# Down products of 16 of 22 hidden tiles as seven products of quadrants, in two passes behind the gates and ups

## The chip, the cores and the metric

The kernel runs on one core of a Trainium2 chip. The metric is device microseconds of one execution, median of three runs. Five engines work side by side, each in the order of its own queue: TensorE (PE, with PEld for its weight loads), VectorE (DVE), ScalarE (ACT), GpSimd (POOL) and SyncE (SP), which issues most DMAs.

## The reference

Two layers over 512 tokens of width 1024; this case is about the feed-forward that ends each.

```python
        h = h + rmsnorm(mixed @ w_out[layer], ln_mix_post[layer])
        f = rmsnorm(h, ln_ffn_pre[layer])
        f = (jax.nn.silu(f @ w_ffn_gate[layer]) * (f @ w_ffn_up[layer])) @ w_ffn_down[layer]
        h = h + rmsnorm(f, ln_ffn_post[layer])
```

D_FF is 2816: 22 hidden tiles of 128. All is float32.

## The kernel before

**Products.** A float32 operand is split into a high part, cast by ACT (L239), and the rest, subtracted by DVE (L240); one product is three matmuls, high by high, low by high, high by low (L182 to L184). A raw weight tile holds 512 KB, four of them are in flight (L134, L157); split weights have eight places.

**Feed-forward.** `boundary` normalizes and turns the rows of h and makes the first two hidden tiles; `combined` (L973) makes the seven sums and parts of the activations. The other 20 tiles come in pairs, in the groups (2,8), (8,14), (14,18), (18,22) of L1093. Gate and up of a pair are one `Seven` each: the two tiles by the two halves of the model and the two halves of the tokens are quadrants, of which seven products, instead of eight, give the result (Strassen-Winograd). A product is 4 k-tiles x 3 matmuls of 256 columns. Four sums of weights (L1022 to L1027) and three of results (L1060 to L1063) are on DVE, four copies out of PSUM on ACT. `gate_rows` (L1108) and `up_rows` (L1114) make silu(gate) x up and split it. After each of the first three groups come its down products (L1164 to L1174), plain: per half of the model and pair of tiles 2 x 4 token blocks x 3 matmuls of 512 columns, added into the eight tiles `ys` (L1174). The last group is done in `tail_of` (L810) token block by token block with the norm that follows.

**Order.** The program order of each engine is the order of its queue; `behind` puts an instruction after others without a wait of its own. SP issues the loads in program order, each when its raw tile is free. POOL has the reciprocal square roots (L253) and four DMAs between attention tiles (L382). PSUM has eight banks under the tags mm (3), lg (3) and tr (2).

Of the kernel before, what the change touches and what calls it, by code (L numbers as in the profile page):

```python
# [7 lines left out]
F32 = mybir.dt.float32  # L8
# [34 lines left out]
def hybrid(ctx: ExitStack, tc: tile.TileContext, i: dict, out: bass.AP):  # L43
# [7 lines left out]
    pp = ctx.enter_context(tc.tile_pool(name="psum", bufs=3, space=PSUM))  # L51

# [78 lines left out]

    def loaded(src):

        raw = wp.tile([P, 1024], F32, tag="raw", name=name("raw"), bufs=4)  # L134
        last_load[0] = nc.sync.dma_start(raw, src)
        return raw
# [182 lines left out]
    h = cp.tile([P, KT, T], F32, name="h")  # L319
# [490 lines left out]
    def tail_of(xs, load, ys, eps=None, last=False):  # L810
# [8 lines left out]
        def tail(tb, halfway=None, ahead=None):  # L819
# [10 lines left out]
            for n, (dh, m0, m1) in enumerate(at):  # L830
# [7 lines left out]
                V.tensor_add(y, o[:, cols], y)  # L838
# [158 lines left out]
    last_sum = [None, None]  # L997

    class Seven:
# [5 lines left out]
        def __init__(self, xs, src, tag, rows):  # L1005
            self.xs, self.rows = xs, rows
            w1, w2 = loaded(src(0)), loaded(src(1))
            self.a = [w[:, d : d + 512] for w in (w1, w2) for d in (0, 512)]
            self.x, self.p = ps(tag, s="x"), ps(tag, (P, 256), s="a")
            self.q = ps(tag, (P, 256), s="e")  # L1010
            self.s1, self.s2 = prob("s1"), prob("s2")

        def parts(self, src):
            pair = pair_of_parts()
            split(src, *pair)
            return pair

        def sums(self):

            a11, a12, a21, a22 = self.a  # L1020
            self.s3 = temp("s3")
            V.tensor_add(self.s3, a11, a21)  # L1022
            self.w1 = self.parts(a11)
            V.tensor_add(a21, a21, a22)
            self.w2 = self.parts(a12)
            V.tensor_add(a11, a21, a11)
            V.tensor_add(a12, a11, a12)  # L1027

        def product(self, o, w, n, more=False):
            for k, w in enumerate(cut(w, P)):  # L1030
                mm3(o, w, self.xs[n][k], k == 0 and not more, k == KT // 2 - 1, more)

        def run(self, what):

            a11, a12, a21, a22 = self.a
            left, right = (slice(*c) for c in HALVES)
            s1, s2 = self.s1, self.s2
            if what == 1:
                self.product(self.p, self.w1, 0)
                A.copy(s1[:, left], self.p)  # L1040
            elif what == 2:
                self.product(self.x[:, left], self.w2, 2)
            elif what == 3:
                self.product(self.x[:, right], self.parts(a12), 5)
            elif what == 4:
                self.product(self.q, self.parts(a22), 4, True)
            elif what == 5:
                self.product(self.p, self.parts(a21), 6, True)
                last_sum[0] = A.copy(s1[:, right], self.p)
            elif what == 6:  # L1050
                self.product(self.p, self.parts(a11), 3, True)
                A.copy(s2[:, left], self.p)
            else:
                self.product(self.q, self.parts(self.s3), 1)
                A.copy(s2[:, right], self.q)

        def end(self):
            left, right = (slice(*c) for c in HALVES)
            s1, s2 = self.s1, self.s2
            V.tensor_add(s2[:, left], self.q, s2[:, left])  # L1060
            V.tensor_add(s2[:, right], self.p, s2[:, right])
            self.rows(1, s2)
            last_sum[1] = V.tensor_add(s1, self.x, s1)  # L1063
            self.rows(0, s1)

    def sevens(pair, plain_first):

        if not plain_first:
            for make in pair:
                u = make()  # L1070
                u.sums()
                for n in (1, 7, 2, 6, 4, 3, 5):
                    u.run(n)
                u.end()
            return
        us = []
        for make in pair:
            us.append(make())
            us[-1].sums()
            for n in (1, 2, 3):  # L1080
                us[-1].run(n)
        for some in ((7, 6), (4, 5)):
            for u in us:
                for n in some:
                    u.run(n)
        for u in us:
            u.end()

    def feed_forward(layer, phase, xp, meanwhile=None):

        nnorm = PairNorm()
        rb = rbc
        groups = ((2, 8), (8, 14), (14, 18), (18, 22))  # L1093
# [11 lines left out]

        gates = [None, None]

        def gate_rows(row, g):  # L1108

            V.tensor_mul(g, g, rb)  # L1110
            A.activation(g, g, AF.Silu, scale=-1.0 if row else 1.0)
            gates[row] = g

        def up_rows(row, u, fs):  # L1114
            if row:
                V.scalar_tensor_tensor(out=u, in0=u, scalar=-1.0, in1=gates[1], op0=ALU.mult, op1=ALU.mult)
# [381 lines left out]
```

## Time and profile before

| what | us |
|---|---|
| three runs | 1113.7, 1114.55, 1115.03 |
| median | 1114.55 |
| span of the profiled execution | 1111.4 |
| PE busy | 1100.8 |
| DVE busy | 893.7 |
| ACT busy | 660.5 |

The profile is of another execution than the runs; its span goes from the first to the last instruction, so it is a few us shorter than a run's time. Each view's times are us from the start of that span. A row of a timeline gives start, duration, engine, line, operation, what it writes and reads, and the shape; a row of the windows the stretch, its length, busy time and count of PE, PEld, DVE, ACT and POOL, granted clock, DMA share and GB/s. The matmul rows overlap: each is longer than the step to the next start.

### The profile page before, as it was taken

The page shows a single profiled execution, that of the slowest core. Times are in us where ns is not written, and L with a number is a line of the kernel's source. Part 1 is how long each engine was busy: PE and PEld are TensorE (multiplying, and loading weights), DVE is VectorE, ACT ScalarE, POOL GpSimd, SP SyncE. Part 2 cuts the span into 40 slices and gives each one's busy share as a digit, 9 for nine tenths or more (in the row PEclk, how much of TensorE's full clock was granted, in tenths as well). Part 3 has the DMA queues.
Part 4 walks back from the last instruction along what each step waited for, and adds up shares of the span by engine and source line. Part 5 has one row for each costly group of instructions (what it writes and reads, how often), then busy time and mean ns, then how long its engine had stood idle before and what let it go on. Part 6 is the DMA issues. An engine that isn't in the chain of part 4 may idle for free.

```text
span 1111.4 us, 19500 instructions
## 1 busy us (share of the span) xinstructions
PE 1100.8 (99%) x7382; PEld 1000.1 (90%) x7382; DVE 893.7 (80%) x1735; ACT 660.5 (59%) x1397; POOL 25.3 (2%) x42
## 2 busy tenths in 40 slices
PE   9999999999999999999999999999999999999997
PEld 7998889998899898998988898889999899899996
DVE  8889658997697597896987898858997697687875
ACT  8776468664365264577665667668665265254553
POOL 0100000000000000001000000000000000000000
PEclk9999999999999999999999999999999999999999
DMA  7522322334133323343322654422224133333222
GB/s 267 162 76 77 98 74 76 115 109 141 57 112 97 117 92 114 97 148 117 104 88 62 173 132 116 131 76 74 79 90 154 62 114 96 101 109 114 77 76 76
DMA packets 64421, 118.12 MB, mean 106 GB/s; under 512 B 5260, under 2 KB 40088, under 8 KB 64328
## 3 DMA queue, kind: packets, MB, share of 16 engines
q1 hardware_dynamic: 63720, 116.18, 33.4%
q8 instruction: 58, 0.95, 0.4%
q0 software_dynamic: 192, 0.52, 0.2%
q14 instruction: 35, 0.29, 0.1%
q10 hardware_dynamic: 416, 0.18, 0.1%
HBM read 104.71 MB, written 2.10 MB: 96 GB/s over the span
## 4 chain that ended last, share of the span: by engine, by line
PE 94%; ACT 3%; DVE 1%; issue 1%; POOL 0%; DMA 0%; POOLq 0%; DVEq 0%; ACTq 0%
PE y L182 10%; PE y L183 10%; PE y L184 10%; PE a L182 5%; PE a L184 5%; PE a L183 5%; PE x L184 3%; PE e L182 3%; PE e L184 3%; PE e L183 3%; PE x L183 3%; PE x L182 3%; PE ps L184 3%; PE ps L183 3%; PE ps L182 3%; PE v L182 2%
## 5 line engine op out<-in xcount | busy, mean ns | idle before, releaser
L239 ACT CAST whi<-raw 128x512 fp32r<-128x512 f32 x460 | 273.1, 620 | 217.7 <-PE y L184 89.1
L240 DVE TENSOR_TENSOR wlo<-raw,whi 128x512 fp32r<-128x512 f32 x460 | 303.5, 684 | 69.5 <-ACT whi L239 67.8
L182 PE MATMUL y<-whi,fhi 128*128 128x512 f32 (+1 forms) x356 | 140.2, 394 | 0.4 <-DVE y L838 0.4
L184 PE MATMUL y<-whi,flo 128*128 128x512 f32 (+1 forms) x356 | 139.3, 391 | 0.0
L183 PE MATMUL y<-wlo,fhi 128*128 128x512 f32 (+1 forms) x356 | 139.2, 391 | 0.0
L184 PE MATMUL x<-xshi,wlo 128*128 128x256 f32 x320 | 89.9, 281 | 0.0
L182 PE MATMUL a<-xshi,whi 128*128 128x256 f32 x320 | 89.8, 281 | 0.0
L183 PE MATMUL x<-xslo,whi 128*128 128x256 f32 x320 | 89.7, 280 | 0.0
L182 PE MATMUL x<-xshi,whi 128*128 128x256 f32 x320 | 89.7, 280 | 0.0
L183 PE MATMUL a<-xslo,whi 128*128 128x256 f32 x320 | 89.7, 280 | 0.0
L184 PE MATMUL a<-xshi,wlo 128*128 128x256 f32 x320 | 89.6, 280 | 0.0
L184 PEld LDWEIGHTS y<-whi,flo 128*128 128x128 f32 x356 | 66.8, 188 | 15.7
L182 PEld LDWEIGHTS y<-whi,fhi 128*128 128x128 f32 x356 | 66.8, 188 | 15.6 <-DVE y L838 0.7
L183 PEld LDWEIGHTS y<-wlo,fhi 128*128 128x128 f32 x356 | 66.9, 188 | 14.7
L182 PEld LDWEIGHTS a<-xshi,whi 128*128 128x128 f32 x320 | 60.2, 188 | 0.5
L183 PEld LDWEIGHTS a<-xslo,whi 128*128 128x128 f32 x320 | 60.2, 188 | 0.3
L184 PEld LDWEIGHTS x<-xshi,wlo 128*128 128x128 f32 x320 | 60.3, 188 | 0.0
L183 PEld LDWEIGHTS x<-xslo,whi 128*128 128x128 f32 x320 | 60.2, 188 | 0.0
L184 PEld LDWEIGHTS a<-xshi,wlo 128*128 128x128 f32 x320 | 60.2, 188 | 0.0
L182 PEld LDWEIGHTS x<-xshi,whi 128*128 128x128 f32 x320 | 60.2, 188 | 0.0
L183 PE MATMUL ps<-xslo,whi 128*128 128x256 f32 x192 | 53.9, 283 | 0.6 <-DVE xslo L240 0.6
L184 PE MATMUL ps<-xshi,wlo 128*128 128x256 f32 x192 | 54.4, 285 | 0.0
(297 smaller groups left out, 3111.1 us busy)
## 6 DMA issues: line engine op xcount, KB each, us to landing
raw<-in_w_gate SPq DMA_DIRECT2D x44, 512.0 KB, 3.5
raw<-in_w_up SPq DMA_DIRECT2D x44, 512.0 KB, 3.6
raw<-in_w_down SPq DMA_DIRECT2D x44, 512.0 KB, 3.8
raw<-in_w_out SPq DMA_DIRECT2D x16, 512.0 KB, 4.8
raw<-in_w_b_q SPq DMA_DIRECT2D x8, 512.0 KB, 3.4
raw<-in_w_a_u SPq DMA_DIRECT2D x6, 512.0 KB
raw<-in_w_v SPq DMA_DIRECT2D x6, 512.0 KB, 4.3
raw<-in_w_k SPq DMA_DIRECT2D x6, 512.0 KB
```

The lines of the kernel that those rows point to most:

```text
L182: PE.matmul(o, w[0], x[0], start=start, stop=False, skip_group_check=more)
L183: PE.matmul(o, w[0], x[1], start=False, stop=False, skip_group_check=more)
L184: return PE.matmul(o, w[1], x[0], start=False, stop=stop, skip_group_check=more)
L239: last_hi[0] = A.copy(hi, src)
L240: last_split[0] = last_hi[0], (eng or V).tensor_sub(lo, src, hi)
```

## The change

Sixteen of the 22 hidden tiles of each layer (2 to 17) go through eight `Down`s, one for each pair. A Down takes quadrants of (two hidden tiles) x (halves of the model), and tokens in halves too: seven products of 2 token blocks x 3 matmuls of 512 columns. Product 2 of a Down is made during the gates and ups of a later pair, into two PSUM banks that are kept over all pairs. When all eight pairs are done, a first pass over the eight Downs adds up products 0, 3, 6 and 5 in PSUM, and a second pass products 1 and 4; `tap` adds the results into `ys` at the end of each pass, `late` during the second. Then come the pairs 18 and 20 and the tail as before, where the right half of the model now has its sign turned.

The float32 hidden rows of the eight pairs must be kept: half of them lie in the place of h, which is stored to DRAM after the boundary and loaded again before the tail. For six gates of the eight pairs, the two last gates and all eight Downs two sums of weights are made in DRAM: SP copies 512 KB from DRAM to DRAM, and a DMA on POOL's queue adds another 512 KB to it (`sums_ahead`). In a `Seven` ACT copies partial results from one PSUM bank to another, where matmuls go on adding; six copies of ACT and one addition of DVE take the place of four and three. Product 3 of a set comes after products 1 and 7 of the next.

```diff
+    hp = ctx.enter_context(tc.tile_pool(name="rows", bufs=1))
+    dp = ctx.enter_context(tc.tile_pool(name="scratch", bufs=1, space=bass.MemoryType.DRAM))
...
+    two_sums, to_sum = {}, []
+    def sums_ahead():
+        if not to_sum:
+            return
+        w, layer, m = to_sum.pop(0)
+        both = two_sums[w, layer, m] = dp.tile([P, 1040], F32, tag=name("sums"), name=name("sums"))[:, :1024]
+        with behind(last_load[0]):
+            if w == "w_down":
+                four = both.rearrange("p (m k c) -> p m k c", m=4, k=2)
+                for dh in range(2):
+                    nc.sync.dma_start(four[:, :, dh, :],
+                                      i[w][layer, 4 * dh : 4 * dh + 4, :, m, :].rearrange("m p c -> p m c"))
+                more = i[w][layer, 4:8, :, m : m + 2, :].rearrange("m p k c -> p m (k c)")
+                G.dma_start(both.rearrange("p (m c) -> p m c", m=4), more, accum_op=ALU.add)
+            else:
+                nc.sync.dma_start(both.rearrange("p (a c) -> p a c", a=2),
+                                  i[w][layer, m : m + 2, :, :512].rearrange("a p c -> p a c"))
+                G.dma_start(both, i[w][layer, m + 1], accum_op=ALU.add)
...
-    h = cp.tile([P, KT, T], F32, name="h")
+    def rows_tile(s, dt=F32):
+        return hp.tile([P, KT, T], dt, tag="h", name=name(s))
+    h = rows_tile("h")
...
-                V.tensor_add(y, o[:, cols], y)
+                (V.tensor_sub if turned_sign and dh else V.tensor_add)(y, o[:, cols], y)
...
+        def __init__(self, xs, w, layer, m, tag, rows, room=None):
+            self.xs, self.tag, self.rows, self.room = xs, tag, rows, room
+            self.parts = {}
+            if (w, layer, m) in two_sums:
+                both, raw = loaded(two_sums[w, layer, m]), loaded(i[w][layer, m])
+                self.s3, self.a21 = both[:, :512], both[:, 512:]
+                self.a22 = temp("a22")
+                nc.sync.dma_start(self.a22, i[w][layer, m + 1, :, 512:])
+                self.summed = True
+            else:
+                raw, more = loaded(i[w][layer, m]), loaded(i[w][layer, m + 1])
+                self.a21, self.a22 = more[:, :512], more[:, 512:]
+                self.summed = False
+            self.a11, self.a12 = raw[:, :512], raw[:, 512:]
+        def form(self, n):
+            a11, a12, a21, a22 = self.a11, self.a12, self.a21, self.a22
+            if n == 7:
+                if not self.summed:
+                    self.s3 = temp("s3")
+                    V.tensor_add(self.s3, a11, a21)
+                    V.tensor_add(a21, a21, a22)
+                return self.s3
+            if n == 6:
+                V.tensor_add(a11, a21, a11)
+            elif n == 3:
+                V.tensor_add(a12, a11, a12)
+            return {1: a11, 2: a12, 3: a12, 4: a22, 5: a21, 6: a11}[n]
+        def product(self, o, x, n, more=False):
             pair = pair_of_parts()
+            split(self.form(n), *pair)
+            for k, w in enumerate(cut(pair, P)):
+                mm3(o, w, self.xs[x][k], k == 0 and not more, k == KT // 2 - 1, more)
+        def run(self, n):
+            left, right = (slice(*c) for c in HALVES)
+            if n == 1:
+                self.p = ps(self.tag, (P, 256), s="a")
+                self.product(self.p, 0, 1)
+                self.x = ps(self.tag, (P, 256), s="x")
+                A.copy(self.x, self.p)
+                self.s1, self.s2 = self.room() if self.room else (prob("s1"), prob("s2"))
+            elif n == 7:
+                self.q = ps(self.tag, s="e")
+                self.product(self.q[:, left], 1, 7)
+                A.copy(self.s2[:, right], self.q[:, left])
+            elif n == 6:
+                self.product(self.p, 3, 6, True)
+                A.copy(self.s2[:, left], self.p)
+            elif n == 4:
+                self.product(self.q[:, left], 4, 4, True)
+            elif n == 2:
+                self.product(self.x, 2, 2, True)
+                A.copy(self.s1[:, left], self.x)
+            elif n == 5:
+                self.product(self.p, 6, 5, True)
+                A.copy(self.q[:, right], self.p)
+                V.tensor_add(self.s2, self.q, self.s2)
+            else:
+                self.product(self.p, 5, 3, True)
+                A.copy(self.s1[:, right], self.p)
+                self.rows(1, self.s2)
+                self.rows(0, self.s1)
...
+    class Down:
+        def __init__(self, layer, k, u0, u1, t):
+            self.layer, self.k, self.u0, self.u1, self.t = layer, k, u0, u1, t
+            self.forms = {}
+            u0, u1, t = self.u0, self.u1, self.t
+            V.tensor_sub(t[:, left], u1[:, right], u0[:, right])
+            V.tensor_sub(u0[:, right], u0[:, left], u0[:, right])
+            V.scalar_tensor_tensor(out=t[:, right], in0=u0[:, right], scalar=-1.0, in1=u1[:, right],
+                                   op0=ALU.mult, op1=ALU.subtract)
+        def last_sum(self):
+            left, right = (slice(*c) for c in HALVES)
+            V.scalar_tensor_tensor(out=self.u1[:, left], in0=self.t[:, right], scalar=-1.0, in1=self.u1[:, left],
+                                   op0=ALU.mult, op1=ALU.subtract)
+        def block(self, dh, x):
+            return i["w_down"][self.layer, 4 * dh : 4 * dh + 4, :, self.k + x, :].rearrange("m p c -> p m c")
+        def weights(self, which):
+            four = lambda t: t.rearrange("p (m c) -> p m c", m=4)
+            sums = four(two_sums["w_down", self.layer, self.k]) if which else None
+            if which == 0:
+                self.a12 = four(temp("a12"))
+                nc.sync.dma_start(self.a12, self.block(0, 1))
+            elif which == 1:
+                raw, t = four(raw_tile()), four(temp("t"))
+                src = i["w_down"][self.layer, :4, :, self.k : self.k + 2, :].rearrange("m p k c -> p m (k c)")
+                last_load[0] = nc.sync.dma_start(raw, src)
+                last_load[0] = nc.sync.dma_start(t, sums[:, :, P:])
+                self.a11, self.a12, self.a21 = raw[:, :, :P], raw[:, :, P:], t
+                raw = raw_tile()
+                self.s3, self.a22 = four(raw[:, :512]), four(raw[:, 512:])
+                last_load[0] = nc.sync.dma_start(self.s3, sums[:, :, :P])
+                last_load[0] = nc.sync.dma_start(self.a22, self.block(1, 1))
+        def product(self, n, o, start, stop):
+            if n == 3:
+                V.tensor_add(self.a11, self.a21, self.a11)
+            elif n == 5:
+                V.tensor_add(self.a12, self.a11, self.a12)
+            src = {0: "a11", 1: "s3", 2: "a12", 3: "a11", 4: "a22", 5: "a12", 6: "a21"}[n]
+            u, c = {0: (self.u0, left), 1: (self.t, left), 2: (self.u1, left), 3: (self.t, right),
+                    4: (self.u1, left), 5: (self.u1, right), 6: (self.u0, right)}[n]
+            both = tp.tile([P, 2, 256], F32R, tag="p", name=name("ff"), bufs=6)
+            split(u[:, c], both[:, 0], both[:, 1])
+            w = pair_of_parts()
+            split(getattr(self, src), *(x.rearrange("p (m c) -> p m c", c=P) for x in w))
+            for t in range(2):
+                tokens = slice(t * P, (t + 1) * P)
+                mm3(o[t], (both[:, 0, tokens], both[:, 1, tokens]), w, start, stop, True)
...
+        kept_h = dp.tile([P, KT, T], F32, tag=name("rows"), name=name("rows"))
+        for k in range(0, KT, 2):
+            nc.sync.dma_start(kept_h[:, k : k + 2, :], h[:, k : k + 2, :])
+        for j in range(2, ones):
+            to_sum.append(("w_gate", layer, 2 + 2 * j))
+            if j > 2:
+                to_sum.append(("w_down", layer, 2 * j - 4))
+        to_sum.extend(("w_gate", layer, m) for m in (18, 20))
+        to_sum.extend(("w_down", layer, m) for m in (12, 14, 16))
+        xs, last = combined(a, scaled, xp)
+        last()
+        ys = [[None] * 2 for _ in range(TB)]
+        kept = [ps("tr", s="x") for _ in range(2)]
+        for tb, dh in [(t, d) for d in (1, 0) for t in range(2)] + [(t, d) for t in (2, 3) for d in range(2)]:
+            o = kept[tb] if tb < 2 and not dh else ps("lg" if dh else "mm", s="y")
+            for k in range(2):
+                token_products(o, fs[k], w[dh][k], tb, k == 0, k == 1)
+            if tb > 1 or dh:
+                ys[tb][dh] = plain("y")
+                A.activation(ys[tb][dh], o, AF.Copy, scale=1.0 - 2 * dh)
+        room = rows_tile("room")
+        downs, gates = [], {}
+        def places():
+            j = len(downs)
+            downs.append(Down(layer, 2 + 2 * j, act("u", F32), room[:, j, :],
+                              act("t", F32) if j < 4 else plain("t")))
+            return downs[j].u0, downs[j].u1
...
+        def up_rows(row, u, some):
             if row:
                 V.scalar_tensor_tensor(out=u, in0=u, scalar=-1.0, in1=gates[1], op0=ALU.mult, op1=ALU.mult)
             else:
                 V.tensor_mul(u, u, gates[0])
+            if some:
+                split(u, *some[row])
+            elif not row:
+                downs[-1].sums()
+        def sets(m, some=None):
+            sums_ahead()
+            yield Seven(xs, "w_gate", layer, m, "mm", gate_rows)
+            sums_ahead()
+            yield Seven(xs, "w_up", layer, m, "lg", lambda row, u: up_rows(row, u, some), None if some else places)
+        def straight(j, last):
+            d = downs[j]
+            d.weights(0)
+            d.product(2, kept, False, last)
+            d.last_sum()
...
+        before = lambda: None
+        for j in range(ones):
+            if j == 0:
+                us = list(sets(2))
+                for n in (1, 2):
+                    for u in us:
+                        u.run(n)
+                for n in (7, 6, 4, 5):
+                    for u in us:
+                        u.run(n)
+                us[0].run(3)
+                before = us[1]
+                continue
+            for n, u in enumerate(sets(2 + 2 * j)):
+                u.run(1)
+                u.run(7)
+                before.run(3)
+                for x in (6, 4, 2, 5):
+                    u.run(x)
+                before = u
+                if n == (j == 1):
+                    straight(j - 1, False)
+        before.run(3)
+        o = {0: [ps("mm", s="p") for _ in range(2)], 3: [ps("lg", s="p") for _ in range(2)]}
+        one, two = [act("ua", F32) for _ in range(2)], [act("ub", F32) for _ in range(2)]
+        def tap(n):
+            for t in range(2):
+                x, y = o[n][t], ys[t]
+                z = ys[2 + t]
+                if n == 0:
+                    A.copy(one[t], x)
+                    V.tensor_add(y[0], x, y[0])
+                elif n == 3:
+                    V.tensor_add(one[t], x, one[t])
+                elif n == 6:
+                    V.tensor_add(two[t], x, one[t])
+                elif n == 5:
+                    V.tensor_add(z[0], x, z[0])
+                elif n == 1:
+                    V.tensor_add(z[1], x, z[1])
+                    V.tensor_add(y[1], x, y[1])
+                else:
+                    V.tensor_add(y[1], x, y[1])
+        for j, d in enumerate(downs):
+            d.weights(1)
+            for n in (0, 3, 5, 6) if j == 0 else (0, 3, 6, 5):
+                if j == 0 and n == 5:
+                    straight(ones - 1, True)
+                    for t in range(2):
+                        ys[t][0] = plain("y")
+                        A.copy(ys[t][0], kept[t])
+                    o[5] = [ps(tag, s="p") for tag in ("mm", "lg")]
+                    o[6] = [ps("tr", s="p") for _ in range(2)]
+                d.product(n, o[n], j == 0, j == ones - 1)
+                if j == ones - 1:
+                    tap(n)
+        o.update({1: [ps("mm", s="q") for _ in range(2)], 4: [ps("lg", s="q") for _ in range(2)]})
+        late = [(z, t, d) for z, d, some in ((2, 0, two), (2, 1, two), (0, 1, one)) for t in range(2)]
+        for j, d in enumerate(downs):
+            d.weights(2)
+            for n in (1, 4):
+                d.product(n, o[n], j == 0, j == ones - 1)
+                if j == ones - 1:
+                    tap(n)
+            if j < len(late):
+                z, t, dh = late[j]
+                y = ys[z + t][dh]
+                V.tensor_add(y, (two if z else one)[t], y)
...
+        h = rows_tile("h")
+        for k in range(0, KT, 2):
+            nc.sync.dma_start(h[:, k : k + 2, :], kept_h[:, k : k + 2, :])
```

**POOL around the boundary of the first layer.** r is a reciprocal square root of the norms, sums the tile in DRAM, before:

```order
15 L253 TENSOR_TENSOR r_1761<-v_1760,mhalf 128x1 x4
16 L253 TENSOR_TENSOR r_3_1765<-var_2233,mhalf 128x2
17 L253 TENSOR_TENSOR r_3_1765<-var_2309,mhalf 128x2
18 L382 DMA memk_6001<-memk_6001 64x512
19 L382 DMA memk_6005<-memk_6005 64x512
```

Now:

```order
15 L281 TENSOR_TENSOR r_1766<-v_1765,mhalf 128x1
16 L181 DMA sums_2517<-in_w_gate 128x1024
17 L281 TENSOR_TENSOR r_1766<-v_1765,mhalf 128x1 x3
18 L281 TENSOR_TENSOR r_3_1770<-var_2238,mhalf 128x2
19 L181 DMA sums_2524<-in_w_gate 128x1024
20 L281 TENSOR_TENSOR r_3_1770<-var_2314,mhalf 128x2
21 L177 DMA sums_2775<-in_w_down 128x4x256
```

Two accumulating DMAs stand between the roots, each waiting for its copy.

**SP at the same place**, from the first down weights on, before:

```order
50 L158 DMA raw_2372<-in_w_down 128x4x256
51 L135 DMA raw_2514<-in_w_gate 128x1024
52 L135 DMA raw_2516<-in_w_gate 128x1024
53 L135 DMA raw_2577<-in_w_up 128x1024
54 L135 DMA raw_2579<-in_w_up 128x1024
```

Now:

```order
50 L186 DMA raw_2377<-in_w_down 128x4x256
51 L179 DMA sums_2517<-in_w_gate 128x2x512
52 L140 DMA raw_2520<-in_w_gate 128x1024
53 L140 DMA raw_2522<-in_w_gate 128x1024
54 L1196 DMA rows_2407<-h_120 128x1024 x2
55 L179 DMA sums_2524<-in_w_gate 128x2x512
56 L1196 DMA rows_2407<-h_120 128x1024 x2
57 L140 DMA raw_2527<-in_w_up 128x1024
58 L140 DMA raw_2529<-in_w_up 128x1024
```

Two copies into sums and the four stores of h (rows) stand ahead of the first up weights.

**DVE between the first and the second pass** of the first layer (ff and wlo are splits, p results in PSUM), now only:

```order
665 L268 TENSOR_TENSOR wlo_5439<-raw_5419,whi_5438 128x512
666 L1286 TENSOR_TENSOR y_4934<-p_4879,y_4934 128x512
667 L1286 TENSOR_TENSOR y_4936<-p_4880,y_4936 128x512
668 L1288 TENSOR_TENSOR ua_4883<-p_4881,ua_4883 128x512
669 L1288 TENSOR_TENSOR ua_4884<-p_4882,ua_4884 128x512
670 L1290 TENSOR_TENSOR ub_4885<-p_4940,ua_4883 128x512
671 L1290 TENSOR_TENSOR ub_4886<-p_4941,ua_4884 128x512
672 L1292 TENSOR_TENSOR y_2487<-p_4938,y_2487 128x512
673 L1292 TENSOR_TENSOR y_2505<-p_4939,y_2505 128x512
674 L1323 TENSOR_TENSOR y_2487<-ub_4885,y_2487 128x512
675 L268 TENSOR_TENSOR ff_5422<-t_2944,ff_5422 128x256
676 L268 TENSOR_TENSOR ff_5435<-room_2516,ff_5435 128x256
```

Eight additions and a late one stand ahead of the splits ff_5422 and ff_5435 of the second pass.

More of the change, by code (lines that the diff above doesn't have):

```diff
@@ L807, in layer_a, with tail_of @@
         return mix_tail(0, mixed, ys)
-    def tail_of(xs, load, ys, eps=None, last=False):
+    def tail_of(xs, load, ys, eps=None, last=False, turned_sign=False):
         ws, tail_split = {}, [None]
@@ L1104, in hidden @@
             split(ff[:, :n], f[0][:, c0:c1], f[1][:, c0:c1])
[L1106 to L1116, printed above, removed]
-            else:
-                V.tensor_mul(u, u, gates[0])
-            split(u, *fs[len(fs) - 2 + row])
         fs = [(act("fhi"), act("flo")) for _ in range(2)]
@@ new lines, in feed_forward @@
+        fs = [(act("fhi"), act("flo")) for _ in range(4)]
+        before = None
+        for m in (18, 20):
+            if meanwhile and m == 20:
+                next(meanwhile)
+            for u in sets(m, fs[m - 18 : m - 16]):
+                u.run(1)
+                u.run(7)
+                if before:
+                    before.run(3)
+                for x in (6, 4, 2, 5):
+                    u.run(x)
+                before = u
+        before.run(3)
+        if meanwhile:
+            next(meanwhile)
```

127 lines of the change are left out of this document (18 added, 109 removed).

## The prediction

> **What bounds the kernel now.** I read the page's first part and its chain of waits, then the waits of TensorE (PE) alone, then windows over a stretch of the feed-forward.
>
> ```profile
> span 1111.4 us, 19500 instructions
> PE 1100.8 (99%) x7382; PEld 1000.1 (90%) x7382; DVE 893.7 (80%) x1735; ACT 660.5 (59%) x1397; POOL 25.3 (2%) x42
> PE 94%; ACT 3%; DVE 1%; issue 1%; POOL 0%; DMA 0%; POOLq 0%; DVEq 0%; ACTq 0%
> q1 hardware_dynamic: 63720, 116.18, 33.4%
> PE yt L871 <- DVE yg L858: 2.3, 1, 2.3
> PE idle L85 <- DVE idle L82: 1.3, 1, 1.3
> PE ps L183 <- DVE xslo L240: 0.6, 2, 0.3
> 205.00:260.00 55.00, 55.00 (x466) 54.94 (x466) 51.92 (x91) 34.48 (x74) 0.00 (x0) 1.00 0.33 105
> 265.00:290.00 25.00, 25.00 (x110) 20.20 (x109) 16.93 (x28) 7.55 (x13) 0.00 (x0) 1.00 0.30 105
> ```
>
> PE is busy 99% of the span and holds 94% of the chain; its longest waits come to a few us, and none lies in the feed-forward. In the two windows (busy PE, weight load, DVE, ACT, POOL; granted clock, DMA share, GB/s) gates and ups (205 to 260) and down products (265 to 290) both fill PE at a granted clock of 1.00. DVE is close behind in the first: 51.92 of 55. So a matmul less saves its own time, as long as DVE (through its weight splits), ACT, DMA and the order on the queues follow.
>
> **The matmuls.** Busy time of a matmul overlaps the next one's, so its cost is the step between starts.
>
> ```profile
> 270.00 0.39 PE L182 MATMUL y<-whi,fhi 128*128 128x512 f32 x1
> ...
> 271.62 0.39 PE L183 MATMUL y<-wlo,fhi 128*128 128x512 f32 x1
> 249.44 0.28 PE L183 MATMUL e<-t,whi 128*128 128x256 f32 x1
> ...
> 250.59 0.28 PE L184 MATMUL x<-xshi,wlo 128*128 128x256 f32 x1
> ```
>
> The first pair of rows is 7 steps apart: 1.62/7 = 0.231 us for 512 columns; the second 10 steps: 1.15/10 = 0.115 us for 256. Gates and ups keep their matmuls: 7 products x 4 x 3 of 256 columns each. Down changes. Two k-tiles took 2 x 2 halves of the model x 4 token blocks x 3 = 48 matmuls of 512 columns; as one Down they take 7 products x 2 token blocks x 3 = 42. Eight Downs in each of two layers: 16 x 6 = 96 fewer, and no kind added. 96 x 0.231 = **22.2 us off PE**. (Taking the busy 0.39 would give 37.4, which is time counted twice.) The Trainium skill, TensorE: Matmul & The Clock Gate, section "Back-to-back issue gap", gives N columns N/2.4 + 2.5 ns, 215.8 ns for 512, by which the saving would be 20.7 us; the rows here step 0.231, and the sum goes by them.
>
> **Does DVE follow?** One step of DVE:
>
> ```profile
> 225.64 0.68 DVE L1116 SCALAR_TENSOR_TENSOR s<-s,s 128x512 f32<-128x512 f32 x1
> 226.24 0.68 DVE L1118 TENSOR_TENSOR s<-s,s 128x512 f32<-128x512 f32 x1
> 224.70 0.43 DVE L1061 TENSOR_TENSOR s<-a,s 128x256 f32<-128x256 f32 x1
> 225.04 0.68 DVE L1063 TENSOR_TENSOR s<-x,s 128x512 f32<-128x512 f32 x1
> 241.46 2.71 ACT L239 CAST whi<-raw 128x512 fp32r<-128x512 f32 x5 [1.51 <-DVE raw L1026]
> 244.07 0.36 ACT L1049 COPY s<-a 128x256 f32<-128x256 f32 x1
> 244.34 0.62 ACT L239 CAST whi<-raw 128x512 fp32r<-128x512 f32 x1
> ```
>
> So 0.60 for 512 columns, 0.34 for 256, estimated 0.40 for a 256-wide form with a scalar; on ACT 0.52 a cast (2.61 to the next start over five) and 0.27 a copy of 256. A pair (gate and up) had 30 of 512 and 4 of 256, 19.4 us against PE's 168 x 0.115 = 19.3: level. Now, from the pair whose gate is summed in DRAM on, product 2 of a Down lies in each pair: PE 19.3 + 6 x 0.231 = 20.7; DVE has 27 of 512 (two sums and two splits of hidden rows fewer, one split of a Down's weight more), and in place of four additions of 256, which ACT's copies take over, three of 256 and two with a scalar for the Down's sums and rows: 16.2 + 1.0 + 0.8 = 18.0. In pass 1 a Down gives PE 24 x 0.231 = 5.5 us and DVE four splits of a weight (512), four of hidden rows (256) and two sums: 4 x 0.94 + 1.2 = 5.0. Pass 2: PE 12 x 0.231 = 2.8, DVE 1.9, or 2.5 with a late addition. ACT: 14 casts and 12 copies a pair, 7.3 + 3.2, and less than 4 of 5.5 in a Down. The new work fits behind PE with 3, 0.5 and 0.3 us to spare; without cover each 512-column DVE instruction would cost 0.60. I price it at **0** in the steady stretches.
>
> **The seams between passes.** At the end of pass 1 eight additions and a late one stand on DVE ahead of the hidden rows that the third product of pass 2 wants. Three of them can only follow the last product: 3 x 0.60 + 0.34 for the split and some 0.3 of latency make it ready 2.4 us behind the end of pass 1, and two products, 2.8 us, come before it: 0 to 1 us. At the start of pass 1 product 2 of the last Down waits for the last up's rows (copy, row, sums, split: some 2 us after the pair's last product), with two products of the first Down, 2.8 us, ahead of it: 0 to 2. Pass 2 to the gate of tile 18: six additions on DVE, 0 to 1. Taken: 0.5 each, **1.5 us a layer**; all together 0 to 4.
>
> **The DMA.** Added per layer: 16 copies inside DRAM of half a MB, 16 accumulating DMAs on POOL's queue, their loads, and h out and in (2 + 2 MB): about 26 MB, so 118 MB become some 170, the share 33% some 50%.
>
> ```profile
> raw<-in_w_gate SPq DMA_DIRECT2D x44, 512.0 KB, 3.5
> raw<-in_w_down SPq DMA_DIRECT2D x44, 512.0 KB, 3.8
> memk<-memk POOLq DMA_DIRECT2D x4, 128.0 KB, 2.7
> L382 POOL DMA_DIRECT2D memk<-memk x4: 518/521/726, 499.3 to 501.0; - x4
> DMA to landing us min/median/max: 2.4/2.7/4.8
> q0 software_dynamic: 192, 0.52, 14.1%
> q1 hardware_dynamic: 1584, 1.57, 32.7%
> ```
>
> Pass 2 wants 512 KB in pieces of 512 bytes every 2.8 us, against pieces of 1 KB now. The last row (window 345 to 360, down weights) gives 0.327 x 16 x 15 / 1584 = 0.050 us for a 1 KB packet. If 512 bytes take as long, 64 of them on each of 16 engines are 3.2 us, if half, 1.6: at worst 0.4 us too slow for each Down, covered by the four loads in advance; **0**, with 0 to 3 a layer as bounds. No row shows an accumulating DMA. On POOL's own queue (row before it, window 498 to 512) 192 packets took 0.141 x 16 x 14 = 31.6 us, 0.164 each of 2.7 KB; half a MB by that rate is 2.0 us of transfer, 3.9 if the target is read as well. Nearest from below is a gate load, 3.5 us; from above the slowest landing of 128 KB four times over, 19.2. They are asked for two pairs ahead (some 40 us), up to 14 behind one another within eight pairs and pass 1: each may take 14.6 us (eight pairs of 20.7 and seven Downs of 5.5, 204 us, over 14) before PE waits. I take 5, nearest the packet rate: **0**; the upper bound would cost 14 x (19.2 - 14.6) = 64 us a layer.
>
> **The boundary.** There POOL makes the reciprocal roots on which the chain hangs, and now two accumulates stand between them, each behind its copy on SP's queue; SP also gets four stores of h and two copies ahead of the first up weights.
>
> ```profile
> 140.58 1.96 SPq L158 DMA_DIRECT2D raw<-in_w_down  x2
> 171.45 1.54 SPq L135 DMA_DIRECT2D raw<-in_w_gate  x2
> 184.95 4.50 SPq L135 DMA_DIRECT2D raw<-in_w_up  x2
> 147.67 0.56 POOL L253 TENSOR_TENSOR r<-v,mhalf 128x1 f32<-128x1 f32 x1 [57.06 <-DVE v L845]
> 153.13 0.56 POOL L253 TENSOR_TENSOR r<-v,mhalf 128x1 f32<-128x1 f32 x1 [4.90 <-DVE v L845]
> 158.65 0.54 POOL L253 TENSOR_TENSOR r<-v,mhalf 128x1 f32<-128x1 f32 x1 [4.97 <-DVE v L845]
> 179.88 0.99 POOL L253 TENSOR_TENSOR r<-var,mhalf 128x2 f32<-128x2 f32 x1 [12.29 <-ACT sq L308]
> 186.01 1.08 POOL L253 TENSOR_TENSOR r<-var,mhalf 128x2 f32<-128x2 f32 x1 [5.14 <-DVE var L283]
> ```
>
> The first copy goes out behind the down weights at 142.5 and, at a load's 3.5 to 5 us, lands before 148; the accumulate then takes 0.52 of POOL and the next root is due at 153.13: **0**, up to 4 a layer if the copy is slow. The second stands between 179.88 and 186.01. Stores of h wait for the last rows of h, and the up weights behind them on SP have from about 185 until the y products that begin at 191 are done, near 202: 0, up to 2.
>
> **Sum**, on the profiled execution: 1111.4 - 22.2 + 2 x 1.5 = 1092.2 of span. The median of the runs, 1114.55, is 3.15 above the span, which I carry over: 1095.3, **1095 us**.
>
> **Rivals.** (1) *Seams and passes cost more*, 4 to 8 us a layer in place of 1.5: DVE takes its queue in order, so that any early addition which waits for a PSUM product holds all splits behind it, and pass 1 has 0.5 us of slack in 5.5. Against it: in the before trace the additions of ys stand among splits too, and PE waits nowhere there. 1100 to 1108. (2) *POOL held at the boundary*: the accumulate waits for its copy in order, and the roots behind it. Each us that the copy lands after about 152 is one of the chain. At 4 us in each layer: 1103. The Trainium skill, DMA: Bandwidth & Descriptors, section "Anatomy of one DMA — SWDGE (gpsimd) path", speaks for it: the receipt can be surprisingly long when HBM is the target; no run so far shows such a write. (3) *The accumulates don't keep up* (the slower side): SP's loads of sums wait for them, and in order behind these all weight loads, PE last. It decides from 14.6 us each, and eats the whole gain at 19.2/28 = 0.7 us more, 15.3. At 16.5 us: 14 x 1.9 x 2 = 53 us, 1148. For it: the 19.2 bound, and copies on the same 16 engines; against it the packet rate, some four times below the limit. (4) *The change saves no matmul*: excluded by the count, 42 against 48.
>
> **How the numbers follow.** Forecast (seams up to 3 us a layer) 0.62; rival 1 0.18; rival 2 0.07; rival 3, or a lesser form of it that leaves little, 0.13, of which 0.09 ends slower and 0.03 about level. A measurement of this kernel can tell 0.2% (2.2 us). Faster: 0.62 + 0.18 + 0.07 and the 0.01 of rival 3 that leaves a gain, less 0.04 for rivals 1 and 2 joined by more than I price: 0.84; of these 0.04 half go to each other side: same 0.05, slower 0.11. The range: no seam costs and no lost step give 1092; a pitch or a stall a little better than read, 1089; above, rivals 1 and 2 to 1109. About 0.16 lies above or below.
>
> **What would show it.** Right: 96 fewer PE matmuls, all of 512 columns; PE busy 1078 to 1080; the steady windows of pairs full at a step of 0.115 and 0.231; DMA near 170 MB. Seams: waits of PE for DVE splits of w_down or of hidden rows around the two pass changes. Rival 2: a root on POOL that starts later behind an accumulate than its input. Rival 3: waits of PE or DVE for a raw tile that holds sums, and accumulates that take over 10 us to land. It would be wrong if DVE in the pairs runs over 20.7 us, or PE steps grow while ACT copies between PSUM tiles.

## The result, and the profile after

The changed kernel takes 1111.79 us (median of 12 runs, 1107.82 to 1115.04) against 1113.42 for the kernel before (12 runs, 1112.56 to 1115.03): ratio 0.9983, 95% interval 0.9973 to 0.9994. It is faster by 1.6 us where 19.5 were forecast. That is less than the 2.2 us that the prediction called the least it could tell, and 1111.79 lies outside its range of 1089 to 1109. Its runs scatter over 7 us, those of before over 2.5.

The page of the profiled execution, with the two DMA queues of section 3 (packets, MB, share of 16 engines' time):

```profile
span 1107.7 us, 19986 instructions
PE 1087.1 (98%) x7286; PEld 985.4 (89%) x7286; DVE 934.4 (84%) x1839; ACT 733.0 (66%) x1609; POOL 59.7 (5%) x74
q1 hardware_dynamic: 114920, 153.93, 45.2%
q0 software_dynamic: 10944, 17.30, 10.0%
PE 79%; DVE 10%; ACT 3%; DMA 3%; issue 3%; SPq 1%; POOL 0%; DVEq 0%; POOLq 0%; ACTq 0%
```

The 96 matmuls are gone (7382 to 7286). But 15% of the chain have gone from PE to DVE, DMA and others, and PE busy fell by 13.7 us, not 22. The waits of PE and of DVE over the whole span say where:

```profile
PE x L212 <- DVE ff L268: 9.4, 10, 1.9
...
DVE s L1055 <- DMA raw<-in_w_up: 22.1, 12, 3.1
```

Ten times PE waits for the split of a Down's hidden rows for product 2 (ff), which is made among the gates and ups; and DVE waits twelve times, 22.1 us in all, for up weights. Windows over gates and ups of the first layer (230 to 340; columns as before), the kernel before first, then the changed one:

```profile
230.00:340.00 110.00, 110.00 (x797) 103.60 (x796) 92.50 (x158) 57.36 (x116) 0.00 (x0) 1.00 0.34 112
```

```profile
230.00:340.00 110.00, 107.70 (x859) 104.94 (x858) 92.07 (x160) 68.76 (x150) 11.07 (x11) 0.98 0.85 219
```

The last two columns: the DMA engines are busy 85% of the time and not 34. (The first stretch has down products in it, so its matmul count does not compare.) One of the ten places in the order of time, DVE first, then PE (start, duration, instruction; in brackets idle time and what ended it):

```profile
246.90 0.69 DVE L1055 TENSOR_TENSOR s<-raw,raw 128x512 f32<-128x512 f32 x1 [2.51 <-DMA raw<-in_w_up]
...
254.31 1.28 DVE L268 TENSOR_TENSOR wlo<-raw,whi 128x512 fp32r<-128x512 f32 x2
255.51 0.42 DVE L268 TENSOR_TENSOR ff<-room,ff 128x256 fp32r<-128x256 f32 x1
```

```profile
253.74 0.39 PE L211 MATMUL x<-wlo,ff 128*128 128x512 f32 x1
255.99 0.50 PE L212 MATMUL x<-whi,ff 128*128 128x512 f32 x1 [1.85 <-DVE ff L268]
```

DVE stands idle 2.51 us for an up weight, then works without a gap, and the split stands behind two weight splits: PE gets it 2 us late.

### The profile page after: what moved, and what is told of

The parts are those of the page before. It is cut to its first block, busy times and chain, and to the rows that moved or that the text cites. A ratio compares the mean times of both kernels' runs of the same rounds, so it can differ in the third digit from the quotient of the medians.

```text
span 1107.7 us, 19986 instructions
## 1 busy us (share of the span) xinstructions
PE 1087.1 (98%) x7286; PEld 985.4 (89%) x7286; DVE 934.4 (84%) x1839; ACT 733.0 (66%) x1609; POOL 59.7 (5%) x74
## 3 DMA queue, kind: packets, MB, share of 16 engines
q0 software_dynamic: 10944, 17.30, 10.0%
HBM read 155.04 MB, written 39.85 MB: 176 GB/s over the span
## 4 chain that ended last, share of the span: by engine, by line
PE 79%; DVE 10%; ACT 3%; DMA 3%; issue 3%; SPq 1%; POOL 0%; DVEq 0%; POOLq 0%; ACTq 0%
PE a L210 5%; PE a L211 5%; PE a L212 5%; DVE wlo L268 5%; PE y L210 4%; PE y L211 4%; PE y L212 4%; PE ps L212 3%; PE ps L211 3%; PE ps L210 3%; PE p L212 3%; PE p L210 3%; PE p L211 3%; PE e L210 2%; PE e L211 2%
## 5 line engine op out<-in xcount | busy, mean ns | idle before, releaser
L210 PE MATMUL a<-xshi,whi 128*128 128x256 f32 x480 | 136.7, 285 | 0.0
L211 PE MATMUL a<-xslo,whi 128*128 128x256 f32 x480 | 136.2, 284 | 0.0
L212 PE MATMUL a<-xshi,wlo 128*128 128x256 f32 x480 | 135.9, 283 | 0.0
L210 PE MATMUL ps<-xshi,whi 128*128 128x256 f32 x192 | 53.7, 287 | 0.0
L210 PE MATMUL y<-whi,mixedhi 128*128 128x512 f32 x128 | 51.6, 403 | 0.0
L211 PE MATMUL y<-wlo,mixedhi 128*128 128x512 f32 x128 | 50.6, 395 | 0.0
L210 PE MATMUL p<-whi,ff 128*128 128x512 f32 x128 | 50.5, 395 | 0.0
L212 PE MATMUL p<-whi,ff 128*128 128x512 f32 x128 | 50.5, 394 | 0.0
L212 PE MATMUL y<-whi,mixedlo 128*128 128x512 f32 x128 | 50.4, 394 | 0.0
L211 PE MATMUL p<-wlo,ff 128*128 128x512 f32 x128 | 50.4, 394 | 0.0
L869 DVE TENSOR_TENSOR y<-y,y 128x512 f32<-128x512 f32 (+1 forms) x33 | 22.2, 673 | 30.4 <-PE y L212 30.3
L210 PE MATMUL e<-t,whi 128*128 128x256 f32 x160 | 45.0, 281 | 0.0
```

The lines of the kernel that those rows point to most:

```text
L210: PE.matmul(o, w[0], x[0], start=start, stop=False, skip_group_check=more)
L211: PE.matmul(o, w[0], x[1], start=False, stop=False, skip_group_check=more)
L212: return PE.matmul(o, w[1], x[0], start=False, stop=stop, skip_group_check=more)
L869: (V.tensor_sub if turned_sign and dh else V.tensor_add)(y, o[:, cols], y)
```

## The experiments

Theory A said that the split stands too late in DVE's order; theory B that DVE is late because up weights land late behind the new DMA traffic. All results beside each other (before: 1113.4 to 1113.7 in each group):

| run | median us | ratio to before, 95% interval |
|---|---|---|
| the change | 1111.8 | 0.9983, 0.9973 to 0.9994 |
| e1 split of the rows earlier | 1107.4 | 0.9945, 0.9928 to 0.9961 |
| e2 no sums made in DRAM | 1094.3 | 0.9829, 0.9814 to 0.9843 |
| e3 both | 1093.2 | 0.9819, 0.9805 to 0.9834 |
| e4 sums made, not read | 1115.1 | 1.0006, 0.9990 to 1.0022 |
| e5 gates' sums on DVE | 1104.6 | 0.9916, 0.9901 to 0.9931 |
| e6 copies only | 1095.8 | 0.9839, 0.9824 to 0.9854 |
| e9 as e5, Downs' sums elsewhere | 1108.8 | 0.9953, 0.9937 to 0.9969 |
| e10 as e9, split earlier | 1102.2 | 0.9885, 0.9865 to 0.9906 |
| e11 plain DMAs for accumulating | 1095.6 | 0.9843, 0.9827 to 0.9860 |
| e12 as e5, split earlier | 1098.3 | 0.9862, 0.9848 to 0.9877 |
| e13 as e11, each twice | 1115.2 | 1.0015, 1.0003 to 1.0027 |
| e15 as e12, split one product later | 1102.6 | 0.9904, 0.9889 to 0.9920 |

e2, e3, e4, e6, e11 and e13 read plain gate weights where sums belong, so they leave out part of the reference; they are there to time the traffic.

**Order or traffic (e1 to e4).** In e1 `rows_of` makes the split, and product 2 later takes it from `forms`:

```diff
+                    if x == 2 and n == (j == 1):
+                        downs[j - 1].forms[2] = downs[j - 1].rows_of(downs[j - 1].u1[:, :256])
                     u.run(x)
```

> The changed kernel with one move: the split of the hidden rows for a Down's product 2 is written ahead of product 2 of the set before it, so that DVE has it two weight splits earlier. In the changed kernel PE waits ten times for this split, 0.3 to 2.0 us each, 10 us in all, and two of the waits are followed by 3.4 us of half clock (1.5 us each). Theory A, the order: the split stands too late on DVE, and moved ahead nearly all of these waits go: about 1099 us where the changed kernel had 1111.8. Theory B, the DMA: DVE itself is late because it is held 1.2 to 2.5 us in each pair by up weights that land late, so the move helps by at most a third of it: 1107 to 1111.

For e2 the body of `sums_ahead` behind the pop is replaced by one line; e3 has both edits; e4 keeps the body and adds the same line at its end:

```diff
+        two_sums[w, layer, m] = i["w_gate"][layer, m]
```

> The changed kernel without the copies and the accumulating DMAs; the loads of the sums read plain gate weights, so half of the products use other weights than they should. Theory B, the DMA: without this traffic up weights land in time, DVE is not held at the first sum of an up, and PE's waits for the split of the rows go: about 1099 us. Theory A, the order: DVE is in time for all but this split, which stays behind two weight splits; half of the waits or more stay: 1104 to 1108.

> Both edits at once, the move of the split and no copies or accumulating DMAs (plain gate weights where the sums are read). Both theories: no wait of PE for the split, no half clock, 1096 to 1099 us. If it is not below the better of the two alone, each alone takes the wait away.

> The changed kernel with its copies and accumulating DMAs as they are, but loads that read plain gate weights in place of the sums, so that none waits for an accumulate; half of the products use other weights than they should. If the traffic on the DMA engines makes the weights late, this stays at the changed kernel's 1110 to 1113 us with the same waits of DVE for up weights. If the loads' wait for the accumulates holds SP's queue, it goes to about the time of the kernel without copies.

The move alone gives 4.4 us: 1107.4 lies at the fast end of theory B's range, far from A's 1099. Without the traffic 17.5 come back, and the move adds 1.1 to that; e2 and e3 end 4.7 and 2.8 us below all that was expected of them. The waits of e1 show that the move shifted the loss rather than ended it:

```profile
PE a L210 <- ACT s L1086: 3.2, 7, 1.0
PE a L210 <- ACT x L1078: 3.2, 10, 0.6
PE e L210 <- ACT room L1083: 3.0, 3, 1.2
...
DVE s L1055 <- DMA raw<-in_w_up: 28.1, 12, 3.2
```

PE now waits for copies of ACT, 9.4 us in 20 waits, and DVE waits for up weights as often as before the move. In e2 that wait is gone but for 1.4 us, and the same window is full:

```profile
230.00:340.00 110.00, 110.00 (x893) 107.87 (x892) 98.97 (x171) 72.83 (x159) 0.00 (x0) 1.00 0.41 126
```

893 matmuls against 859, with the same DVE work a pair as in the change: DVE can follow. e4 is no faster than the change (1115.1, even above its 1110 to 1113), so no load waits in earnest for its sum; it is the traffic by itself.

**Which traffic (e5, e6).** e5 drops the two lines that put gates into `to_sum`; e6 is e4 without the two accumulating DMAs.

```diff
-            to_sum.append(("w_gate", layer, 2 + 2 * j))
...
-        to_sum.extend(("w_gate", layer, m) for m in (18, 20))
```

> The changed kernel with half of the sums in DRAM: those of the Downs stay, those of the gates go back to two additions on DVE. Copies and accumulates fall from 32 of each to 16. The cost of all of them was 1111.8 - 1094.3 = 17.5 us. If the traffic costs by its bytes, half of it comes back: 1103. If it is the second sum of a pair that is too much, most of it: 1096 to 1099. Rival, DVE: with 1.2 us more a pair (19.2 of PE's 20.7) DVE is late by itself, and the time stays above 1106.

> The changed kernel with the copies inside DRAM and without the accumulating DMAs; the loads of the sums read plain gate weights, so half of the products use other weights than they should. The accumulates took 10.0% of the 16 engines, the copies some 4.6% (q1 45.2% against 40.6% without them). By that share the copies alone cost a third of 17.5 us: 1100. If the copies, which stand on SP's own queue ahead of the weights, do it all: 1109 to 1112. If the accumulates do: 1094 to 1096.

The copies cost 1.5 us (1095.8 against 1094.3), the accumulates the other 19 of e4.

e5 gets 7 us back, but it does not show what one sum a pair would cost. `sums_ahead` is still called twice a pair, so the Downs' sums go out as fast as before and only end earlier: the first layer's last accumulate is issued at 259.70, where the changed kernel has it at 348.59. The DMA share is 0.96 from 220 to 240 and 0.89 from 240 to 260, and 0.30 to 0.50 in the stretches of 20 us from there to 340. All eight waits of PE for ff come after the last accumulate of their layer. The windows 855 to 945, where e5 makes no sums, of e2 first, then of e5, and its waits for ff:

```profile
855.00:945.00 90.00, 90.00 (x738) 88.47 (x737) 79.69 (x137) 59.60 (x131) 0.00 (x0) 1.00 0.42 133
855.00:945.00 90.00, 86.64 (x700) 84.13 (x700) 81.16 (x140) 56.62 (x123) 0.00 (x0) 1.00 0.39 117
...
PE x L212 <- DVE ff L268: 5.5, 8, 1.1
```

With no more DMA traffic than e2, e5 loses 3.4 us of PE there, on a DVE with more to do. So a good part of what e5 still loses is the rival of its expectation, DVE, together with the late split, though not up to the 1106 named there.

**The sums made at another time (e9, e10).** e9 is e5 with the Downs' sums of both layers in `to_sum` from the start, one taken behind each load of the output projection, none in `sets`:

```diff
+        parts = moving_pair(i["w_out"][layer, 4 * dh : 4 * dh + 4, :, 256 * kp : 256 * kp + 256]
+                            .rearrange("m p c -> p m c"), aside)
+        sums_ahead()
+        return parts
```

> The changed kernel with no traffic of sums among gates and ups: the gates' sums on DVE, and the eight sums of a layer's Downs made earlier, one behind each load of the output projection's weights. If what costs is traffic while up weights are loaded just in time, this has nearly the time without any sums in DRAM: 1094 to 1098. If 1.2 us more on DVE in each pair is too much, 1100 or more. If the copies and accumulates hold the loads of the output projection or POOL's roots instead, the loss shows up there and the time is 1100 to 1106.

> The same with the split of the hidden rows for product 2 moved ahead. If DVE is in time, nothing comes from it (the pair of kernels without any sums differed by 1.1 us): 1093 to 1097. If DVE is late in the pairs, this gains 2 to 4 us on the kernel beside it.

e9 falls on the branch of a DVE with too much to do (1100 or more), above the ranges of the others; e10 gains 6.6 us on it, more than either branch had. In e10 the pairs are full (897 matmuls in the window), but PE waits elsewhere, in the attention of the second layer, whose own transfers go through the same engines:

```profile
PE lg L528 <- DMA qc<-whi: 4.2, 1, 4.2
```

Behind this wait PE runs at a granted clock of 0.52 (window 680 to 685), which takes 2.4 of these 5 us; with the wait that is 6.6 of the 9.4 us by which e10's span is longer than e2's. e9 waits at the same line, 4.2 us in 3 waits. Moved traffic met another transfer that is needed at once. The 6.6 us from e9 to e10 are the late split again, on a fuller DVE: the DMA share in e9's window is only 0.39.

**The adding, or the engines' time (e11, e13).**

```diff
-                G.dma_start(both, i[w][layer, m + 1], accum_op=ALU.add)
+                first = G.dma_start(both, i[w][layer, m + 1])
+                with behind(first):
+                    G.dma_start(other, i[w][layer, m + 1])
```

(and the same for w_down; e11 has only the first of the two; the loads read plain weights as in e4.)

> The changed kernel with a plain DMA of the same size and shape on POOL's queue in place of each accumulating one; the loads of the sums read plain gate weights, so half of the products use other weights than they should. It is to be compared with 1115.1 (the same with accumulates) and 1095.8 (copies alone). If the adding is what costs (an accumulate's packets took 10.0% of 16 engines for 17.3 MB, 0.162 us each of 1.6 KB, where those of loads took 0.070 of 1.3 KB), the plain DMA costs at most a third of it: 1096 to 1102. If any traffic on POOL's queue does it, or the bytes, 1108 to 1115.

> The kernel with plain DMAs on POOL's queue in place of the accumulating ones, and each of them issued twice, the second into another tile in DRAM; the loads of the sums read plain gate weights, so half of the products use other weights than they should. Twice 15.8% of the engines' time in the pairs is what the accumulates took there (31.4%), so that the engines are as full as with them (85 to 90%). If the time that an accumulate's packets hold the engines is what makes the up weights late, this is slow too: 1108 to 1118. If it is something else in the adding, it stays near the 1095.6 of one plain DMA: 1095 to 1099.

These two decide between the adding and the engines' time. The two queues over the whole span and the window, first e11, then e13:

```profile
q0 software_dynamic: 4800, 17.30, 5.0%
...
230.00:340.00 110.00, 110.00 (x892) 107.82 (x891) 98.77 (x171) 72.68 (x158) 6.48 (x10) 1.00 0.75 232
```

```profile
q0 software_dynamic: 9408, 34.08, 9.4%
...
230.00:340.00 110.00, 105.56 (x852) 102.63 (x852) 91.31 (x158) 68.83 (x150) 12.89 (x20) 1.00 0.84 266
DVE s L1061 <- DMA raw<-in_w_up: 24.9, 12, 3.6
```

Plain DMAs of the same bytes take half the engines' time of the accumulating ones (5.0% against 10.0%) and cost nothing. Issued twice they fill the engines as accumulates do, DVE waits for up weights as with these (24.9 us, 12 times), and the time is the same, 1115.2 against 1115.1. So the loss needs neither the adding nor the use of POOL's queue as such: it comes with the time for which the engines are held. It is not the bytes either, which the pages count alike for e4 and e11 (HBM read 155.04 MB, written 39.85). The number of packets on POOL's queue grows along with the time (4800, 9408, and 10944 with accumulates); the two were not parted.

The share of the window climbs from 0.41 without sums (e2) to 0.60 with the copies (e6), 0.75 with plain DMAs on POOL's queue (e11) and 0.85 in the change. At 0.75 DVE waits 4.9 us in all for up weights and PE not at all for ff; at 0.84 PE waits. Where between the two the loss begins was not tried, and a share is no threshold by itself: in e12 below it is 0.98 and 0.91 from 220 to 240 and from 240 to 260, with PE busy all the time. The Trainium skill, DMA: Bandwidth & Descriptors, section "Queues, rings and completion order", says that each DMA engine takes turns between its queues, a packet at a time. e13 agrees in so far as traffic on POOL's queue delays loads on SP's (24.9 us of waits); the turns themselves no run here shows.

**A version faster than both kernels (e12, e15).** e12 has the edits of e5 and e1; e15 puts the early split at `x == 5`, which comes after 2 in the order of products.

> The changed kernel with the gates' sums on DVE, the Downs' sums in DRAM one a pair as before, and the split of the hidden rows moved ahead. Its parts gave 1104.6 and 1107.4 alone. If the traffic of one sum a pair does no harm and what is left in the first of them is the place of the split on DVE, the waits go: 1095 to 1099. If one accumulate a pair still makes up weights late, 1101 to 1104.

> The kernel with the gates' sums on DVE and the split of the hidden rows moved ahead (1098.3), with the split written one product later, ahead of product 5 in place of product 2. What is left there are waits of PE for ACT's copies that stand behind the early cast of the split, some 3 us. If the cast holds them: 1095 to 1097. If what is left comes from accumulates that make up weights late: 1098 to 1100.

e12 at 1098.3, within its first range, is the fastest that computes the whole reference: half of the traffic, and the split early. Its sums still go out two a pair in the first pairs, as in e5, and not one a pair as its expectation has it; a kernel with one a pair was not run. One product later (e15) PE waits for the rows again, 3.9 us in 7 waits: 1102.6, above both of its expectations.

## Why the prediction was wrong

- **The matmuls:** right in count and nearly in worth. With the traffic gone the time is 1094.3, where 1095 were forecast, and PE busy 1080.8 where 1078 to 1080 were. That these times agree so well is partly luck: the span of e2 saves 19.3 us (1111.4 to 1092.1), not 22.2, and the missing 2.9 are not at the seams, for which 3 had been priced, but in many matmul steps a little longer than before, 2.8 us when summed over the kernel.
- **DVE follows:** right as far as work goes (forecast 18.0 of 20.7 us a pair; in e2 98.97 of 110, with PE full). What was left out is that DVE is in order and is held by a load.
- **The seams:** taken as 1.5 us a layer; PE has no wait at either change of pass in the profile after. The y products ahead of the first gates start 0.95 us later than before (192.42 and 191.47), but so does the 223rd matmul (37.96 and 36.97), long before the boundary, where POOL's roots keep their distances: rival 2 did not happen.
- **The DMA:** this step failed. It priced the accumulates at 0; copies and accumulates together cost 17.5 us (1111.8 in the change, 1094.3 in e2), nearly all of it the accumulates' (1095.8 in e6). The 0 came of asking when they would be late for their own reader, with 14.6 us each as the limit. They landed in 6.3 and 7.3 us at the median, none later than 9.8, above the 5 assumed but well within the limit:

```profile
raw<-in_w_up SPq DMA_DIRECT2D x10, 512.0 KB, 4.9
sums<-in_w_down POOLq DMA_DIRECT2D x6, 512.0 KB, 7.3
...
sums<-in_w_gate POOLq DMA_DIRECT2D x5, 512.0 KB, 6.3
```

  (the changed kernel's window 230 to 340.) What it did not ask is what they do to the loads beside them. The share was worked out over the whole kernel (50%; it became 55), but the traffic lies in the pairs, where it is 85%. An up load landed in 4.9 us there and in 3.4 without the traffic, and it is issued only when a raw tile comes free (SP's loads of L140 wait 77 times for a split of DVE), so that a delay of it is passed on to DVE, whose twelve waits are 1.8 us each. In e13 the up loads landed in 3.7 and the gate loads in 4.9, so the delay is not that of one load alone; how it adds up from load to load was not traced. The price itself was in the text, 3.9 us of transfer a sum if the target is read too (measured: 10.0% of 1107.7 us over 32 sums, 3.5 us of all 16 engines); two of them a pair, with copies and loads, were never added up against the pair's 20.7 us.
- **Rival 3** named the right traffic with the wrong mechanism: it had SP held by the sums' loads, and e4 shows that this costs nothing.
- **Rival 1** had the last link right, work that PE needs queued behind other work on DVE, but put it at the passes and gave it the wrong cause.

The 18.5 us between the matmuls' 22.2 and the span's 3.7 are, in the profiled execution: 11 us in the ten waits (counted between starts of matmuls, above the step), 3 us of half clock behind two of them, 0.9 from the start, and some 3 in gaps under 0.15 us that I did not assign and that e2 has too. All ten waits for the split are gone in e1 as in e2, but only e2 brings the time back: in the changed kernel the order sets where PE waits, the traffic that it waits.

A small one: the 3.15 us between span and median were carried over, where the profiled run of the changed kernel is 1109.39 for a span of 1107.7, 1.7.

## What to carry to other kernels

When work goes to DMA, add up the engines' time of all transfers within the stage in which they run, not over the kernel, and ask which load there is issued just in time; a transfer that is on time for its own reader can still make that load late. Price an accumulating DMA inside DRAM at twice a plain one's engine time (10.0% against 5.0% here). A split that PE needs early should be written early: behind two others on an engine in order, it turns a small delay of one load into a wait of PE. And when an experiment takes half of some traffic away, look whether its rate fell or only its end came sooner.

## What was not expected of the hardware

A stall of PE of 2.2 us between two starts can cost 1.5 us beyond its own length. After the one at 255.99 and another at 884.19 PE ran at half speed for 3.4 us, beginning 1.1 to 1.2 us after work had resumed:

```profile
257.69 0.41 PE L211 MATMUL a<-xslo,whi 128*128 128x256 f32 x1
257.90 0.41 PE L212 MATMUL a<-xshi,wlo 128*128 128x256 f32 x1
...
260.79 0.28 PE L212 MATMUL e<-t3hi,wlo 128*128 128x256 f32 x1
260.90 0.28 PE L210 MATMUL e<-t3hi,whi 128*128 128x256 f32 x1
256.00:260.00 4.00, 4.00 (x19) 3.82 (x20) 3.27 (x6) 1.15 (x3) 0.84 (x1) 0.65 0.65 200
```

Steps of 0.21 us in place of 0.115, some 1.5 us lost each time; the granted clock of the window is 0.65. Stalls of up to 2.0 us between two starts, as in e4 at 278.01, had no such sequel in any run here (the last 30 us, with little work for PE, left aside). Of eight of 2.24 to 2.35 us four had it: the two of the change, one of two in e4, one of three in e13, and not the one in e9. The Trainium skill, TensorE: Matmul & The Clock Gate, section "Part 1: The HAM clock gate", puts the drop after an idle window of some 3.4 us; here 2.2 us between two starts were enough, so the measurement decides. The scatter of the changed kernel's runs does not follow from this: the fastest and the slowest, 1107.82 and 1115.04, have the same mean granted clock, 0.994. Its cause is open.
